# Hybrid decoder layer: eleven weight subtractions moved to GpSimd, a one-column product written as another instruction, a minimum folded into the reduction before it

## The chip, the core and the metric

The kernel runs on one core of one Trainium2 chip. The metric is the device time in microseconds (us) of one execution. The kernel before took a median of 1356.11 us in three runs (1355.26 to 1356.71); less is better. A core has five engines that work side by side and meet by semaphores: TensorE (PE in the profile; its weight loads have a row of their own, PEld), VectorE (DVE), ScalarE (ACT), GpSimd (POOL) and SyncE (SP, which only issues DMAs here). Each takes its instructions in a fixed order.

## The reference, cut to what matters

One decoder layer on 1024 tokens of width 1024, in float32. The part that the change touches:

```python
xn = rmsnorm(x, norm_mix_w[l])
proj = xn @ w_in[l]
da_q, da_k, da_v, sw_q, sw_k, sw_v, g_da, g_sw = split_cols(proj)
y_da = diff_attention(da_q, da_k, da_v, lam, lam_init, subln_w[l])
y_sw = sliding_window_attention(sw_q, sw_k, sw_v, sinks[l])
merged = sigmoid(g_da) * (y_da @ w_br_da[l]) + sigmoid(g_sw) * (y_sw @ w_br_sw[l])
x = x + merged @ w_mix_out[l]
...
# diff_attention, per head and block of 128 queries: two softmaxes, then
a = p[:, :, 0] - lam * p[:, :, 1]
# sliding_window_attention, per group of 4 heads: window of 128 keys plus a sink logit
p = softmax(concatenate([logits, sink], axis=-1), axis=-1)[..., :-1]
```

After it come a gated feed-forward part with a causal convolution and a last normalisation, which the change does not touch.

## The kernel before, in words

Every large matrix product is done in three passes on numbers split in two: a weight block `raw` of 128x1024 comes by DMA, ScalarE copies its high part `wh` (L129), VectorE subtracts to get the low part `wl` (L131), and TensorE then runs high x high, high x low and low x high (L150 to L152). `load_w` does the loading and splitting; `ahead` takes the next entry of a list of sources made in `plan` and calls it, so that a block is split one block ahead of its use. An entry may carry a third element, the engine of the subtraction; without one it is VectorE.

The input projection has 34 column blocks. Two gate blocks are done early and three in pairs; the last eleven gate blocks (23 to 33) are kept back and computed during attention: `back_half` runs one half (128x512) of one block, 24 matmuls, copies it to SBUF and stores it to DRAM (L494 to L498). Which halves follow which attention step is written out by hand in `HALVES`. They give TensorE something to do while the softmaxes run.

Attention has six units. Units 0 to 3 are the differential heads, each of eight steps (`da_step`): step i forms the scores of 128 queries against (i+1)x128 keys for two score maps (L568), adds the distance bias and takes the row minimum in one custom VectorE instruction (L572, followed by an instruction that reads out its accumulator), exponentiates on ScalarE (L573), forms the factor of the second map from a reciprocal and a one-column product (L576, L577), subtracts the maps on VectorE (L578), transposes the result on TensorE in groups of up to four blocks (L584) and splits it (ScalarE L586, VectorE L587). Every second step `da_av` multiplies with the values (L596 to L598). `da_norm` leaves the head's normalisation to the next unit's steps: L616 to L620 and the transposes of L173. Score tiles, transpose tiles and gate tiles have two buffers each in PSUM, so L568 can write a score tile only when the L572 two tiles before has read it, and L584 a transpose tile only when L587 (or ScalarE's copy) has read the one two before.

Units 4 and 5 are the sliding window in groups of four heads (`sw_step`, 8 steps each): scores (L656), bias and row minimum for each of the heads (L659), the minimum with the negated sinks (L661), the sink's distance from it (L662), exponentials (L663, L665), sum and reciprocal (L666, L667), normalising (L670: three heads on VectorE, the fourth on GpSimd), transposes (L677), splitting (L680, L681), product with the values (L687), and L689 to L694 to gather the result. GpSimd otherwise clears score tiles (L551), takes the -1/2 power (L167) and does L620 in this stretch; before it and after it, it does large products and sums (L385, L725).

The order in which one engine gets its instructions is not that of the source: the framework's scheduler orders them when the program is built, from dependencies, buffers, priorities and its own cost estimates; so single gate matmuls stand among those of the attention. After that the order is fixed. SP's queue issues the loads, among them the next `raw` (L119), which waits until one of three buffers has been read.

Of the kernel before, what the change touches and what calls it, by code (L numbers as in the profile page):

```python
# [13 lines left out]
ALU = mybir.AluOpType  # L14
# [6 lines left out]
KC = D // P  # L21
# [21 lines left out]
class Trunk:  # L43
# [173 lines left out]
    def plan(self):  # L217

        self.kind = {m: "q" if m < 4 or 12 <= m < 16 else "k" if m < 8 or m == 16 else "v" if m < 18 else "g" for m in range(34)}


        self.plain = [0, 4, 8, 18, 20]
        self.pairs = [(1, 5), (9, 2), (6, 10), (3, 7), (11, 12), (13, 16), (17, 14), (15, 19), (21, 22)]
        gates = list(range(23, 34))
        self.back = []
        todo = [(m, hf) for m in gates for hf in range(2)]
        for steps in HALVES:
            self.back.append([[todo.pop(0) for _ in range(n)] for n in steps])
        assert not todo
        src = [(self.w_in[m], KC) for m in self.plain]  # L230
        src += [((self.w_in[a], self.w_in[b]), "pair") for a, b in self.pairs]
        src += [(self.w_in[m], KC) for m in gates]
        src += [(self.w_br[m], KC) for m in range(KC)]
        self.mix_order = [m for k in range(4) for m in (k, k + 4)]
        src += [(self.w_mix[m], KC) for m in self.mix_order]
        src += [((self.w_up[j], self.w_up[j + NF]), "pair") for j in range(NF)]


        n, n2 = N1 // 2, NF - N1 - 8
        self.pieces = [(m, c) for m0 in (4, 0) for c in range(2) for m in range(m0, m0 + 4)]  # L240
        src += [(self.w_dn[m:m + 2, :, n * c:n * c + n, :].rearrange("m p k c -> p m k c"), 2 * n) for m, c in self.pieces[::2]]
        pairs = [(self.w_dn[m, :, N1:N1 + 8, :], self.w_dn[m + 4, :, N1:N1 + 8, :]) for m in range(4)]
        src.insert(len(src) - 2, (pairs[0], "sums"))
        src += [(self.w_dn[m, :, N1:N1 + 8, :], 8) for m in range(4)]
        src += [(pairs[0], "rest")] + [(p, "pair", True, 1) for p in pairs[1:]]
        src += [(self.w_dn[m, :, N1 + 8:, :], n2) for _ in range(2) for m in range(KC)]
        self.wsrc, self.wq, self.deep = src, [], False
# [306 lines left out]
    def da_step(self, h, i, st, aT):  # L554
        nc, ap = self.nc, self.ap
        q, k = st
        slope = 4.0 ** -(h + 1)
        w = (i + 1) * P

        lo = P if w == 640 else 0  # L560
        cuts = ((0, 256),) if i == 0 else ((0, w),) if w <= H2 else ((0, H2 - lo), (H2 - lo, w))
        pr = []
        for c in range(2):
            sc = self.tl(self.psS, [P, T], "sc")
            qs = q[c][:, i * P:(i + 1) * P]
            for part in range(2):
                for n0, n1 in cuts:
                    nc.tensor.matmul(sc[:, lo + n0:lo + n1], qs, k[c][part][:, n0:n1], start=part == 0, stop=part == 1)  # L568
            L = self.tl(ap, [P, T], "L", bufs=4)
            s = self.tl(self.st, [P, 4], "sm", bufs=8)  # L570
            o = 896 - i * P
            nc.vector.tensor_tensor_reduce(L[:, :w], sc[:, lo:lo + w], self.bias[:, o:o + w], slope, 3e38, ALU.add, ALU.min, s[:, 0:1])  # L572
            nc.scalar.activation(L[:, :w], L[:, :w], AF.Exp, bias=s[:, 0:1], scale=-1.0, accum_out=s[:, 1:2] if c else self.s0[:, i:i + 1])  # L573
            pr.append(L)

        nc.vector.reciprocal(s[:, 2:3], s[:, 1:2])  # L576
        nc.vector.tensor_scalar(s[:, 3:4], self.s0[:, i:i + 1], s[:, 2:3], self.neglam, ALU.mult, ALU.mult)  # L577
        nc.vector.scalar_tensor_tensor(pr[0][:, :w], pr[1][:, :w], s[:, 3:4], pr[0][:, :w], ALU.mult, ALU.add)  # L578
        qo = (i % 2) * P
        for j0 in range(0, i + 1, 4):  # L580
            nj = min(4, i + 1 - j0)
            ps = self.tl(self.psT, [P, 4, P], "t")
            for j in range(nj):
                nc.tensor.transpose(ps[:, j, :], pr[0][:, (j0 + j) * P:(j0 + j + 1) * P], self.ident)  # L584
            hi, lo = aT[j0 // 4, 0], aT[j0 // 4, 1]
            nc.scalar.copy(hi[:, :nj, qo:qo + P], ps[:, :nj, :])  # L586
            nc.vector.tensor_tensor(lo[:, :nj, qo:qo + P], ps[:, :nj, :], hi[:, :nj, qo:qo + P].bitcast(F32), ALU.subtract)  # L587
# [57 lines left out]
    def sw_step(self, g, n, st):  # L645
        nc, ap = self.nc, self.ap
        q, k = st
        k0 = max(n - 1, 0) * P
        w = P if n == 0 else 256
        bo = T + (P if n == 0 else 0)  # L650
        sc = self.tl(self.psS, [P, 4, 256], "sc")
        s = self.tl(self.st, [P, 4, 4], "sw", bufs=4)
        L = self.tl(ap, [P, 4, 256], "L", bufs=4)
        for h in range(4):
            for part in range(2):
                nc.tensor.matmul(sc[:, h, :], q[h][:, n * P:(n + 1) * P], k[part][:, k0:k0 + 256], start=part == 0, stop=part == 1)  # L656
        for h in range(4):
            slope = 2.0 ** -(4 * g + h + 1)
            nc.vector.tensor_tensor_reduce(L[:, h, :w], sc[:, h, :w], self.bias[:, bo:bo + w], slope, 3e38, ALU.add, ALU.min, s[:, 0, h:h + 1])  # L659
        sink = self.vecs[:, C_SINK + 4 * g:C_SINK + 4 * g + 4]  # L660
        nc.vector.tensor_tensor(s[:, 0, :], s[:, 0, :], self.nsink[:, 4 * g:4 * g + 4], ALU.min)  # L661
        nc.vector.tensor_tensor(s[:, 1, :], s[:, 0, :], sink, ALU.add)  # L662
        nc.scalar.activation(s[:, 1, :], s[:, 1, :], AF.Exp)  # L663
        for h in range(4):
            nc.scalar.activation(L[:, h, :w], L[:, h, :w], AF.Exp, bias=s[:, 0, h:h + 1], scale=-1.0, accum_out=s[:, 2, h:h + 1])  # L665
        nc.vector.tensor_tensor(s[:, 2, :], s[:, 2, :], s[:, 1, :], ALU.add)  # L666
        self.last = nc.vector.reciprocal(s[:, 3, :], s[:, 2, :])  # L667
        for h in range(4):
            eng = nc.gpsimd if h in (3,) else nc.vector
            eng.tensor_scalar(L[:, h, :w], L[:, h, :w], s[:, 3, h:h + 1], None, ALU.mult)  # L670
        po = self.tl(self.psT, [P, H2], "t")
        nblk = w // P
        parts = []
        for b in range(nblk):
            ps = self.tl(self.psT, [P, 4, P], "t")
            for h in range(4):
                nc.tensor.transpose(ps[:, h, :], L[:, h, b * P:(b + 1) * P], self.ident)  # L677
            pt = self.tl(ap, [P, 2, 4, P], "aT", F32R, bufs=5)
            hi, lo = pt[:, 0], pt[:, 1]
            nc.scalar.copy(hi, ps)  # L680
            nc.vector.tensor_tensor(lo, ps, hi.bitcast(F32), ALU.subtract)  # L681
            parts.append((hi, lo))
        for b, (hi, lo) in enumerate(parts):
            kb = k0 // P + b
            va = self.vsw[kb // 4][:, kb % 4, g]
            for m, pt in enumerate((hi, lo)):
                nc.tensor.matmul(po, va, pt, start=b == 0 and m == 0, stop=b == nblk - 1 and m == 1)  # L687
        t = self.tl(self.gpool, [P, 4, P], "g", bufs=2)[0:64]
        nc.scalar.copy(t, po[64:128].rearrange("p (h q) -> p h q", h=4))  # L689
        pv = po[0:64].rearrange("p (c e q) -> p c e q", c=2, e=2)  # L690
        tv = t.rearrange("p (c e) q -> p c e q", e=2)
        y = self.tl(ap, [P, 2, P], "ys", bufs=3)
        for e in range(2):
            nc.vector.tensor_tensor(y[64 * e:64 * e + 64], pv[:, :, e], tv[:, :, e], ALU.add)  # L694
        self.store(self.yd[4 + 2 * g:6 + 2 * g, :, n * P:(n + 1) * P].rearrange("c p q -> p c q"), y)
# [515 lines left out]
```

## Time and profile before

| | |
|---|---|
| median of three runs | 1356.11 us (1355.26 to 1356.71) |
| the profiled execution | 1356.2 us, of which 1354.3 us are the span of its instructions |
| granted TensorE clock | 0.996 of full speed |
| busy over the span | PE 1335.0 us (99%), DVE 1009.8 us (75%), ACT 603.9 us (45%), POOL 483.1 us (36%) |

Times in the profile are counted from the span's first instruction. In a timeline row stand the start, the busy time, the engine, the source line, the operation with the tile it writes and those it reads, their shapes and how many instructions are merged into the row; in brackets the idle time of the engine before it and what ended that. In a table of stretches stand first and last time, length, and then for each engine its busy time with the number of instructions. In a row of a group stand the form, the count, the busy time of all and the mean in ns of one. A TensorE instruction's end is modelled, and one overlaps the next, so its starts say more than its busy time.

### The profile page before, as it was taken

Reading aid. Unit: us, or ns where it says so; the run is one execution under the profiler, and the core shown is the slowest. Engines: PE = TensorE matmul, PEld = TensorE weight load, DVE = VectorE, ACT = ScalarE, POOL = GpSimd, SP = SyncE. Lnnn points to the kernel's source line nnn. Section 1 sums busy time; section 2 is a strip of 40 time slices with the busy share of each in tenths; the row PEclk is TensorE's granted clock in tenths of the full one; section 3 lists DMA queues with packets and bytes.
Section 4 is the critical chain, followed back from the end, with each engine's and each line's share of the span. In section 5 each row is a group of like instructions: output and inputs, shape, how many; then the busy total and the mean of one; then the engine's idle time right before and its main releaser. Section 6 shows DMA issues by size and latency. Waiting matters only on the chain.

```text
span 1354.3 us, 17160 instructions
## 1 busy us (share of the span) xinstructions
PE 1335.0 (99%) x6304; PEld 1103.6 (81%) x6304; DVE 1009.8 (75%) x1454; ACT 603.9 (45%) x942; POOL 483.1 (36%) x350
## 2 busy tenths in 40 slices
PE   7999999999999999999999999999999999999997
PEld 6888888888887777878888888888888888888886
DVE  8846775388898875355689888888888898986454
ACT  8422232376667664334444334433443345433343
POOL 0436651010102125741455565555555611231011
PEclk9999999999999999999999999999999999999999
DMA  6334443966554235334422222122212248651342
GB/s 255 140 113 164 143 156 114 272 174 175 156 133 144 77 116 219 117 119 136 166 82 88 71 91 94 62 79 93 93 63 83 92 141 311 215 177 64 94 134 85
DMA packets 62470, 179.50 MB, mean 133 GB/s; under 512 B 6833, under 2 KB 15153, under 8 KB 62385
## 3 DMA queue, kind: packets, MB, share of 16 engines
q1 hardware_dynamic: 50928, 160.98, 36.7%
q10 hardware_dynamic: 11456, 17.41, 3.5%
q8 instruction: 50, 0.82, 0.2%
q14 instruction: 36, 0.29, 0.1%
HBM read 129.61 MB, written 48.76 MB: 132 GB/s over the span
## 4 chain that ended last, share of the span: by engine, by line
PE 62%; DVE 17%; POOL 7%; issue 7%; DMA 4%; ACT 3%; POOLq 0%; DVEq 0%; SPq 0%; ACTq 0%
PE t L836 7%; PE t L837 7%; PE t L835 7%; POOL us L965 3%; PE y L996 3%; PE d L996 3%; PE sc L568 3%; PE g L150 2%; PE g L151 2%; DVE c L958 2%; PE g L152 2%; DVE wl L112 2%; DMA gr<-gd 2%; PE sc L151 2%; PE sc L152 2%
## 5 line engine op out<-in xcount | busy, mean ns | idle before, releaser
L970 ACT ACTIVATE c<-us,vecs 128x1024 f32<-128x1024 f32 x44 | 54.8, 1248 | 163.2 <-POOL us L965 160.0
L965 POOL TENSOR_TENSOR us<-us,rstd 128x1024 f32<-128x1024 f32 x42 | 100.7, 2414 | 52.8 <-DVE wl L131 34.3
L110 ACT CAST sh<-sf 128x1024 fp32r<-128x1024 f32 x62 | 64.9, 1051 | 106.2 <-POOL sf L97 61.8
L129 ACT CAST wh<-raw 128x1024 fp32r<-128x1024 f32 (+2 forms) x60 | 60.7, 1012 | 104.8 <-PE sc L151 33.1
L971 DVE SCALAR_TENSOR_TENSOR c<-us,vecs,c 128x1024 f32<-128x1024 f32 x44 | 67.1, 1527 | 51.9 <-ACT c L970 51.9
L131 DVE TENSOR_TENSOR wl<-raw,wh 128x1024 fp32r<-128x1024 f32 (+2 forms) x60 | 75.3, 1256 | 39.1 <-ACT wh L129 29.3
L96 POOL TENSOR_TENSOR sf<-rv 128x512 f32<-128x512 f32 x30 | 42.5, 1417 | 166.7 <-DMA rv<-in_w_up 73.2
L112 DVE TENSOR_TENSOR sl<-sf,sh 128x1024 fp32r<-128x1024 f32 x62 | 88.3, 1426 | 8.2 <-ACT sh L110 8.2
L167 POOL TENSOR_TENSOR rs<-ms,mhalf 128x8 f32<-128x8 f32 (+2 forms) x9 | 14.5, 1614 | 159.1 <-DVE ms L165 148.5
L150 PE MATMUL g<-xh,wh 128*128 128x512 f32 x176 | 70.7, 402 | 0.1
L152 PE MATMUL g<-xh,wl 128*128 128x512 f32 x176 | 70.4, 400 | 0.0
L151 PE MATMUL g<-xl,wh 128*128 128x512 f32 x176 | 70.4, 400 | 0.0
L98 POOL TENSOR_TENSOR sf<-raw,rv 128x512 f32<-128x512 f32 x30 | 41.6, 1386 | 59.9 <-DVE sl L112 59.9
L572 DVE CUSTOM_DVE_ANT_0 L<-sc,bias 128x128 f32<-128x128 f32 (+7 forms) x64 | 47.7, 752 | 17.4 <-PE sc L568 14.1
L551 POOL MEMSET aT<- 128x128 f32 x32 | 6.1, 204 | 152.0 <-PE t L597 101.6
L573 ACT ACTIVATE L<-L,sm 128x128 f32<-128x128 f32 (+7 forms) x64 | 49.6, 778 | 20.7 <-DVE sm L572 18.2
L97 POOL TENSOR_TENSOR sf<-sf,raw 128x512 f32<-128x512 f32 x31 | 58.0, 1870 | 1.6
L972 DVE SCALAR_TENSOR_TENSOR c<-us,vecs,c 128x1024 f32<-128x1024 f32 x44 | 56.2, 1279 | 0.6
L725 POOL TENSOR_TENSOR gr<-gr,rstd 128x1024 f32<-128x1024 f32 x16 | 39.4, 2467 | 41.4 <-DMA gr<-gd 41.2
L112 DVE TENSOR_TENSOR wl<-raw,wh 128x1024 fp32r<-128x1024 f32 (+1 forms) x35 | 52.8, 1508 | 0.1
L151 PE MATMUL sc<-ml,wh 128*128 128x512 f32 x128 | 50.1, 391 | 0.6 <-DVE ml L746 0.6
L568 PE MATMUL sc<-u,u 128*128 128x512 f32 (+2 forms) x192 | 49.8, 359 | 0.1
(444 smaller groups left out, 4351.4 us busy)
## 6 DMA issues: line engine op xcount, KB each, us to landing
u<-qd SPq DMA_DIRECT2D x72, 256.0 KB, 6.1
raw<-in_w_down SPq DMA_DIRECT2D x27, 512.0 KB, 3.7
raw<-in_w_in SPq DMA_DIRECT2D x25, 512.0 KB, 4.4
hr<-hd SPq DMA_DIRECT2D x50, 256.0 KB, 5.3
raw<-in_w_up SPq DMA_DIRECT2D x23, 512.0 KB, 3.6
hd<-c SPq DMA_DIRECT2D x22, 512.0 KB, 2.8
rv<-in_w_up SPq DMA_DIRECT2D x21, 512.0 KB, 3.5
gr<-gd SPq DMA_DIRECT2D x16, 512.0 KB, 3.6
```

What stands on the lines that cost most here:

```text
L112: nc.vector.tensor_tensor(lo, src, hi.bitcast(F32), ALU.subtract)
L131: self.lo = (eng or nc.vector).tensor_tensor(wl, raw, wh.bitcast(F32), ALU.subtract)
L150: nc.tensor.matmul(ps, wh[:, kc + o, :], ah, start=first and n == 0, stop=False)
L151: nc.tensor.matmul(ps, wh[:, kc + o, :], al, start=False, stop=False)
L152: nc.tensor.matmul(ps, wl[:, kc + o, :], ah, start=False, stop=last and n == len(kcs) - 1)
L568: nc.tensor.matmul(sc[:, lo + n0:lo + n1], qs, k[c][part][:, n0:n1], start=part == 0, stop=part == 1)
L835: nc.tensor.matmul(ps, ah[:, k, :], bh, start=first and n == 0, stop=False, skip_group_check=skip)
L836: nc.tensor.matmul(ps, ah[:, k, :], bl, start=False, stop=False, skip_group_check=skip)
L837: nc.tensor.matmul(ps, al[:, k, :], bh, start=False, stop=last and n == len(ks) - 1, skip_group_check=skip)
L965: i = (nc.vector if m % NF == 0 else nc.gpsimd).tensor_tensor(us[:, 2:], us[:, 2:], self.rstd, ALU.mult)
L971: nc.vector.scalar_tensor_tensor(c, us[:, 1:T + 1], cw[1], c, ALU.mult, ALU.add)
L996: nc.tensor.matmul(ps, v[:, n, :], x, start=n == i == 0, stop=n == len(js) - 1 and i == 2)
```

## The change

Three edits. The list entries of the eleven gate blocks name GpSimd as the engine of the subtraction at L131. The one-column product at L577, until now a `tensor_scalar` of one column with two per-partition scalars, becomes a `scalar_tensor_tensor` of two columns with one such scalar. And the reduction at L659 gets the column of the negated sink as the value its minimum begins with, in place of the constant 3e38, and the separate minimum at L661 goes.

```diff
-        src += [(self.w_in[m], KC) for m in gates]
+        src += [(self.w_in[m], KC, self.nc.gpsimd) for m in gates]
...
-        nc.vector.tensor_scalar(s[:, 3:4], self.s0[:, i:i + 1], s[:, 2:3], self.neglam, ALU.mult, ALU.mult)
+        nc.vector.scalar_tensor_tensor(s[:, 3:4], self.s0[:, i:i + 1], self.neglam, s[:, 2:3], ALU.mult, ALU.mult)
...
-            nc.vector.tensor_tensor_reduce(L[:, h, :w], sc[:, h, :w], self.bias[:, bo:bo + w], slope, 3e38, ALU.add, ALU.min, s[:, 0, h:h + 1])
+            nc.vector.tensor_tensor_reduce(L[:, h, :w], sc[:, h, :w], self.bias[:, bo:bo + w], slope, self.nsink[:, 4 * g + h:4 * g + h + 1], ALU.add, ALU.min, s[:, 0, h:h + 1])
         sink = self.vecs[:, C_SINK + 4 * g:C_SINK + 4 * g + 4]
-        nc.vector.tensor_tensor(s[:, 0, :], s[:, 0, :], self.nsink[:, 4 * g:4 * g + 4], ALU.min)
```

## The prediction

> **What bounds the kernel now.** I read the page first, then the table of stretches over attention, then the moved line in the same stretches, then the timelines at the places that it leads to.
>
> ```profile
> span 1354.3 us, 17160 instructions
> PE 1335.0 (99%) x6304; PEld 1103.6 (81%) x6304; DVE 1009.8 (75%) x1454; ACT 603.9 (45%) x942; POOL 483.1 (36%) x350
> ...
> 223.00:266.00 43.00, 42.91 (x196) 35.38 (x195) 12.53 (x22) 8.04 (x13) 0.85 (x5) 1.00 0.79 234
> 266.00:397.00 131.00, 130.93 (x832) 114.66 (x831) 114.92 (x298) 90.43 (x211) 10.81 (x33) 1.00 0.60 160
> 397.00:497.00 100.00, 98.17 (x552) 79.17 (x551) 85.95 (x315) 70.25 (x207) 17.53 (x18) 1.00 0.35 106
> ```
>
> The columns after the length are PE, PEld, DVE, ACT and POOL, then the granted clock and the DMAs. PE sets the time. In the four differential heads (266 to 397) it is idle 0.07 us, in the sliding window (397 to 497) 1.83 us. VectorE is second, busy 88% and 86% there, GpSimd idle almost throughout. So relief for VectorE pays only where PE stands waiting for it, and a delay of VectorE costs as soon as it exceeds its lead over PE.
>
> The same stretches for L131 alone (the last one ends before the first block of w_br, which stays on VectorE):
>
> ```profile
> 223.00:266.00 43.00, 4.90 (x4) 1.00 0.79 234
> 266.00:397.00 131.00, 4.88 (x4) 1.00 0.60 160
> 397.00:493.00 96.00, 3.62 (x3) 1.00 0.34 105
> ```
>
> These are the eleven: 1.22 us each, four in a stretch where VectorE is busy 12.53 of 43 us, four among the heads, three in the window.
>
> **Part one, the subtraction on GpSimd.** What does a 128x1024 operation with two inputs in SBUF cost there, and what does it do to VectorE?
>
> ```profile
> 198.36 2.41 POOL L385 TENSOR_TENSOR us<-us,rstd 128x1024 f32<-128x1024 f32 x1 [0.52 <-DVE us L401]
> 198.45 3.40 DVE L112 TENSOR_TENSOR sl<-sf,sh 128x1024 fp32r<-128x1024 f32 x1 [0.17 <-ACT sh L110]
> ```
>
> GpSimd takes 2.41 us. The VectorE subtraction that starts 0.09 us after it has the form of L131, 1.22 us, but takes 3.40: it ends at 201.85, which is GpSimd's end (200.77) plus 1.08. So a VectorE operation that reads two SBUF tensors does not run beside such a GpSimd operation; it waits for its end and then runs whole. The other way round too:
>
> ```profile
> 476.83 1.20 DVE L131 TENSOR_TENSOR wl<-raw,wh 128x1024 fp32r<-128x1024 f32 x1
> 477.11 1.71 POOL L670 TENSOR_SCALAR L<-L,sw 128x256 f32<-128x256 f32 x1 [9.19 <-DVE sw L667]
> 479.70 0.99 POOL L670 TENSOR_SCALAR L<-L,sw 128x256 f32<-128x256 f32 x1 [0.88 <-PE t L677]
> ```
>
> GpSimd's L670 takes 1.71 us behind L131 and 0.99 without. So a moved subtraction takes 1.22 us off VectorE and can hold it for up to 2.41 if one of its two-input operations comes up meanwhile (L578, L617, L662, L666): from 1.22 us early to 1.19 late for each.
>
> The first four cost nothing: VectorE is idle 71% of that stretch, which is the cover; without it each would fall under the bounds just given. For the heads I place the hold in the trace. GpSimd can start when ScalarE's copy of `wh` ends. Second of the four:
>
> ```profile
> 321.82 1.07 ACT L129 CAST wh<-raw 128x1024 fp32r<-128x1024 f32 x1
> 322.53 1.15 DVE L578 SCALAR_TENSOR_TENSOR L<-L,sm,L 128x896 f32<-128x896 f32 x1
> 323.60 0.16 DVE L617 TENSOR_TENSOR r<-r 128x8 f32<-128x8 f32 x1
> 323.67 1.22 DVE L131 TENSOR_TENSOR wl<-raw,wh 128x1024 fp32r<-128x1024 f32 x1
> 324.88 0.27 DVE L572 CUSTOM_DVE_ANT_0 L<-sc,bias 128x128 f32<-128x128 f32 x1
> 325.49 0.40 PE L568 MATMUL sc<-u,u 128*128 128x256 f32 x2
> ```
>
> The copy ends at 322.89, in the middle of L578; GpSimd gets in when that ends, about 323.6, and holds until 326.0. Next on VectorE is L617, eight columns wide, but with two SBUF inputs: it waits. It ends at about 326.1 where L131 ended at 324.89, and L572 follows 1.2 late, reading its score tile until 326.4. L568 at 325.49 writes the tile that this L572 frees: PE stands about 1.0 us, and behind it in PE's order stand gate matmuls that were ready. The third:
>
> ```profile
> 358.54 1.07 ACT L129 CAST wh<-raw 128x1024 fp32r<-128x1024 f32 x1
> 359.19 1.28 DVE L578 SCALAR_TENSOR_TENSOR L<-L,sm,L 128x1024 f32<-128x1024 f32 x1
> 360.39 0.16 DVE L617 TENSOR_TENSOR r<-r 128x8 f32<-128x8 f32 x1
> 360.47 1.22 DVE L131 TENSOR_TENSOR wl<-raw,wh 128x1024 fp32r<-128x1024 f32 x1
> 361.60 1.15 DVE L587 TENSOR_TENSOR aT<-t,aT 128x512 fp32r<-128x512 f32 x2
> 362.66 0.60 PE L584 MATMUL t<-ident,L 128*128 128x128 f32 x4
> ```
>
> The same pattern: hold from 360.4 to 362.8, L617 behind it, L587 from 361.60 to about 362.9, and the transposes at 362.66, which need the tile that the first L587 frees (361.60 plus half of 1.15), 1.2 late. The fourth:
>
> ```profile
> 392.18 1.15 DVE L578 SCALAR_TENSOR_TENSOR L<-L,sm,L 128x896 f32<-128x896 f32 x1
> 393.62 0.15 DVE L617 TENSOR_TENSOR r<-r 128x8 f32<-128x8 f32 x1
> 396.41 1.28 DVE L578 SCALAR_TENSOR_TENSOR L<-L,sm,L 128x1024 f32<-128x1024 f32 x1
> 397.87 1.04 PE L584 MATMUL t<-ident,L 128*128 128x128 f32 x8
> ```
>
> Hold from 393.3 to 395.7, L617 ends 2.1 late of which the missing L131 returns 1.2: L578 ends 0.9 late, at 398.6 instead of 397.69, and the transposes at 397.87 wait 0.7. The first of the four I take as even: a hold that begins anywhere takes half of 2.41 on average, and 1.22 is saved. Heads together: 0 + 1.0 + 1.2 + 0.7 = +2.9 us; bounds -0.1 (PE's idle time there, all of it) and 4 x 1.19 = +4.8.
>
> In the window:
>
> ```profile
> 434.16 0.35 DVE L670 TENSOR_SCALAR L<-L,sw 128x256 f32<-128x256 f32 x1
> 434.83 1.29 DVE L670 TENSOR_SCALAR L<-L,sw 128x256 f32<-128x256 f32 x3
> 434.99 0.99 POOL L670 TENSOR_SCALAR L<-L,sw 128x256 f32<-128x256 f32 x1 [1.69 <-PE t L677]
> 436.05 1.21 DVE L131 TENSOR_TENSOR wl<-raw,wh 128x1024 fp32r<-128x1024 f32 x1
> 437.18 1.28 DVE L681 TENSOR_TENSOR aT<-t,aT 128x512 fp32r<-128x512 f32 x2
> 492.42 1.28 PE L677 MATMUL t<-ident,L 128*128 128x128 f32 x4 [0.27 <-DVE L L670]
> ```
>
> Here GpSimd's L670 is done at 435.98, the subtraction follows until 438.4, and VectorE's next work is L681, whose one input is in PSUM: no hold, 1.2 us gained. PE's waits for VectorE are at places like the last row: four transposes in 1.28 us where four take 0.60 above, and 0.27 idle before. GpSimd's own L670 may queue up to 2.41 behind a subtraction, with the transposes L677 waiting for it; GpSimd is busy 17.53 of 100 us, so for three blocks I take 0.
>
> A rule against even that, row first: three L670 beside GpSimd's L670 took 1.29 us, 0.43 each against 0.35 alone; none waited for GpSimd's end at 435.98, or the last would end at 436.7 instead of 436.12. The Trainium skill (SBUF — State Buffer, "Who interferes with whom") counts VectorE's `tensor_scalar` in its two-port fast mode among what a GpSimd instruction blocks for its whole length; by it the sum would be 3.6 higher (below). The row decides against it for a one-input GpSimd instruction; no row shows a two-input one.
>
> **Part two, L577.** In the heads:
>
> ```profile
> L577 DVE TENSOR_SCALAR sm<-s,sm,neglam 128x1 f32<-128x1 f32 x32 | 8.7, 271 | 0.3
> L587 DVE TENSOR_TENSOR aT<-t,aT 128x512 fp32r<-128x512 f32 x22 | 14.9, 687 | 2.2 <-ACT aT L586 2.1
> L578 DVE SCALAR_TENSOR_TENSOR L<-L,sm,L 128x512 f32<-128x512 f32 x4 | 3.0, 746 | 0.0
> ```
>
> L578 has one per-partition scalar more than L587 and takes 59 ns more at equal size: I price such a scalar at 59. The new L577 has two columns and one scalar: the four-column two-input L661 below (158) plus 59 is 217, so 54 less, 32 times: 1.7 us off VectorE (bounds 0 and 32 x (271 - 158) = 3.6). It lies on the chain to L578, but PE idles 0.07 us: I take -0.1. The new form has two SBUF inputs, so it too can be held.
>
> **Part three, the minimum.** In the window:
>
> ```profile
> L659 DVE CUSTOM_DVE_ANT_0 L<-sc,bias 128x256 f32<-128x256 f32 x56 | 21.7, 418 | 1.6 <-PE sc L656 1.6
> L661 DVE TENSOR_TENSOR sw<-sw,nsink 128x4 f32<-128x4 f32 x16 | 2.5, 158 | 0.1
> ```
>
> 16 x 158 = 2.5 us go; 64 reductions (56 and 8 narrower) gain a scalar, 64 x 59 = 3.8 (bounds 0 and twice that, 7.6). VectorE pays 1.3. What is gained is a wait: a head's exponential need no longer wait for all four heads and L661, only for its own reduction.
>
> Window together: VectorE loses 3.6 and gets 1.3 back, and the chain is shorter; of PE's idle 1.83 I take it all, and nothing of what overlapping matmuls hide: -1.8, with bounds -4.5 (as much again, and the 0.95 of the last row) and +3.6 (three holds of 1.2). No queue is passed by a DMA; SP's `raw` load waits for the subtraction's end, which moves by at most 1.2 late and often early, with blocks split over 10 us ahead.
>
> **Sum:** +2.9 - 0.1 - 1.8 = +1.0 on the profiled execution's own 1356.2 (1354.3 of span, 1.9 around it), which is 0.1 above the median of the runs: 1357.1 us.
>
> **The rivals.**
> - Faster: the scheduler's new order puts the holds beside one-input operations (in the heads L572 and L587 are most of VectorE's time). For it: the window's rows; against it: L578 and L617 follow each other at every place that I looked at. Then 0 - 0.1 - 3.6 (twice the idle) = -3.7: 1352.5.
> - Slower: one mechanism, the hold, at all seven dense blocks, each at its full 1.19, with VectorE's lead gone so that PE pays all: 8.3 - 0.1 = +8.2, 1364.4. It decides once more than about four of the seven meet a two-input operation early. For it: each step has several (L578, L617, the new L577; L662, L666); against: the window's rows at 436.
> - The page's rule as a mechanism: a GpSimd subtraction stops the fast L670 too, in all three window blocks: 1357.1 + 3 x 1.2 = 1360.7.
> - Nothing on PE's path changes: holds and gains vanish in PE's order, 1356.2.
>
> **How the numbers follow.** A measurement of this kernel tells 0.2%, 2.7 us, from no change. Forecast 0.42 (own range 1354.5 to 1360: 0.02 faster, 0.32 same, 0.08 slower); faster 0.22 (0.18 faster, 0.04 same); slower 0.20; the page's rule 0.08 (0.02 same, 0.06 slower); nothing 0.08 (same). Together faster 0.20, same 0.46, slower 0.34. The range leaves out half of the slower rival and the far end of the faster: 1352 to 1362.5.
>
> **What would show it.** L131 on GpSimd at 2.4 us each; in the heads L617, L578 or L577 lengthened to up to 2.4 us behind it, and PE's busy time in the heads below all but 0.1; L577 near 217 ns; L659 near 477; PE's idle time in the window smaller. It is wrong if no VectorE row is lengthened beside the new subtractions, if L659 keeps 418, or if PE's order changes so much that waits of other kinds appear.

## The result, and the profile after

The changed kernel takes a median of 1362.51 us in six runs (1360.42 to 1365.5), the kernel before 1356.41 us in six runs on the same chip (1355.26 to 1357.39): ratio 1.0047, 95% interval [1.0034, 1.006], so 6.1 us slower. The profiled execution took 1363.76 us with a span of 1361.9. Of its source, the lines behind L661 have a number one smaller than before (L669 is before's L670, L686 its L687).

The head of the page of the changed kernel, and two stretches of attention with the columns explained above:

```profile
span 1361.9 us, 17127 instructions
...
PE 1335.7 (98%) x6304; PEld 1102.0 (81%) x6304; DVE 1011.0 (74%) x1427; ACT 604.0 (44%) x942; POOL 511.2 (38%) x361
```

```profile
266.00:397.00 131.00, 128.26 (x798) 109.81 (x797) 113.16 (x290) 87.63 (x207) 19.43 (x36) 1.00 0.58 156
397.00:505.00 108.00, 104.75 (x600) 85.51 (x599) 90.28 (x302) 74.46 (x213) 26.25 (x23) 1.00 0.36 107
```

TensorE does the same 6304 instructions in about the same busy time (1335.7 against 1335.0 us). What has grown is its idle time: 2.74 us among the heads where it was 0.07, and 3.25 us in the window where it was 1.83. VectorE has the 27 instructions less that the diff takes away (x1427 against x1454) but a busy time 1.2 us larger, so something on it runs longer. What TensorE waited for from 223 to 505 us (us in total, number of waits, longest), first in the changed kernel, then in the kernel before:

```profile
PE sc L568 <- DVE sm L572: 2.4, 2, 1.5
PE sc L568 <- DMA u<-qd: 1.5, 1, 1.5
PE t L686 <- DVE aT L680: 1.4, 1, 1.4
PE t L686 <- DVE v L643: 1.1, 1, 1.1
PE g L150 <- ACT g L497: 0.6, 1, 0.6
```

```profile
PE t L687 <- DVE aT L681: 0.4, 2, 0.2
PE t L677 <- DVE L L670: 0.4, 2, 0.3
PE t L677 <- POOL L L670: 0.2, 1, 0.2
```

Waits of 1.0 us in all have become 7.0, five of those in the three lines where VectorE is late. All in all TensorE is idle 7.5 us from 223 to 505 us where it was idle 2.0; that is 5.5 of the 7.6 us between the two profiled spans. The single prices are as predicted. All instructions of a line in the changed kernel, with minimum, median and maximum in ns:

```profile
L577 DVE SCALAR_TENSOR_TENSOR sm<-s,neglam,sm x32: 208/216/2373, 270.3 to 396.9; 128x1 f32<-128x1 f32 x32
L659 DVE CUSTOM_DVE_ANT_0 L<-sc,bias,nsink x64: 324/475/485, 400.2 to 496.8; 128x256 f32<-128x256 f32 x56, 128x128 f32<-128x128 f32 x8
L131 POOL TENSOR_TENSOR wl<-raw,wh x11: 2370/2389/2557, 226.9 to 478.8; 128x1024 fp32r<-128x1024 f32 x11
```

The maximum of L577 stands out, eleven times its median. The timeline of the changed kernel at four of the eleven subtractions says why:

```profile
291.21 2.56 POOL L131 TENSOR_TENSOR wl<-raw,wh 128x1024 fp32r<-128x1024 f32 x1 [0.39 <-ACT wh L129]
291.45 2.34 DVE L617 TENSOR_TENSOR r<-r 128x8 f32<-128x8 f32 x1
294.05 0.51 PE L568 MATMUL sc<-u,u 128*128 128x256 f32 x2 [0.92 <-DVE sm L572]
331.95 2.38 POOL L131 TENSOR_TENSOR wl<-raw,wh 128x1024 fp32r<-128x1024 f32 x1 [4.41 <-ACT wh L129]
331.97 2.37 DVE L577 SCALAR_TENSOR_TENSOR sm<-s,neglam,sm 128x1 f32<-128x1 f32 x1
408.72 2.37 POOL L131 TENSOR_TENSOR wl<-raw,wh 128x1024 fp32r<-128x1024 f32 x1 [3.94 <-ACT wh L129]
409.10 2.03 DVE L165 TENSOR_SCALAR ms<-r 128x8 f32<-128x8 f32 x1
436.42 2.37 POOL L131 TENSOR_TENSOR wl<-raw,wh 128x1024 fp32r<-128x1024 f32 x1
436.94 2.00 DVE L669 TENSOR_SCALAR L<-L,sw 128x256 f32<-128x256 f32 x1
```

Each of these VectorE instructions begins while GpSimd subtracts and ends when GpSimd ends: 291.45 + 2.34 is 293.79, GpSimd's end 293.77. Alone, L617 takes 0.16 us and L670 0.35. The two waits for L572 and those for L643 and L680 in the list above follow just behind these four places (TensorE's next instruction starts at 294.05, 335.1, 411.9 and 439.6). A fifth, an L577 at 369.24, is held for 1.26 us. The two last of those shown are not of the kind that the prediction counted as held: L165 and L669 are `tensor_scalar`, with one input in SBUF.

But the hold was not the whole difference. Set side by side, some 575 of TensorE's 6304 matmuls stand in another place of its order than before, all of them between 269 and 519 us, in attention and just behind it, although no edit touches TensorE. So there were three theories: the **order** (the scheduler, given other costs and another engine for eleven instructions, made another order for all engines), the **hold** (GpSimd's subtractions stop VectorE), and SyncE's **late load** (the `raw` load waits for the longer subtraction, and the loads queued behind it, among them that of `u`, come late: the 1.5 us of L568 above).

### The profile page after: what moved, and what is told of

Read it like the earlier page. It is cut to its first block, busy times and chain, and to the rows that moved or that the text cites. A ratio compares the mean times of both kernels' runs of the same rounds, so it can differ in the third digit from the quotient of the medians.

```text
span 1361.9 us, 17127 instructions
## 1 busy us (share of the span) xinstructions
PE 1335.7 (98%) x6304; PEld 1102.0 (81%) x6304; DVE 1011.0 (74%) x1427; ACT 604.0 (44%) x942; POOL 511.2 (38%) x361
## 4 chain that ended last, share of the span: by engine, by line
PE 66%; DVE 18%; issue 6%; POOL 4%; DMA 3%; ACT 2%; POOLq 0%; SPq 0%; DVEq 0%; ACTq 0%
PE t L836 6%; PE t L835 6%; PE t L834 6%; POOL us L964 4%; PE y L995 3%; PE d L995 3%; PE g L151 3%; PE g L152 3%; PE g L150 3%; PE sc L152 3%; PE sc L150 3%; PE sc L151 3%; DVE wl L112 3%; DVE c L957 2%; PE sc L568 2%
## 5 line engine op out<-in xcount | busy, mean ns | idle before, releaser
L131 DVE TENSOR_TENSOR wl<-raw,wh 128x1024 fp32r<-128x1024 f32 (+2 forms) x49 | 64.1, 1309 | 23.8 <-ACT wh L129 23.5
L150 PE MATMUL g<-xh,wh 128*128 128x512 f32 x176 | 70.4, 400 | 0.6 <-ACT g L497 0.6
L151 PE MATMUL g<-xl,wh 128*128 128x512 f32 x176 | 70.7, 402 | 0.0
L152 PE MATMUL g<-xh,wl 128*128 128x512 f32 x176 | 70.3, 399 | 0.0
L572 DVE CUSTOM_DVE_ANT_0 L<-sc,bias 128x128 f32<-128x128 f32 (+7 forms) x64 | 47.7, 753 | 21.0 <-PE sc L568 18.1
L724 POOL TENSOR_TENSOR gr<-gr,rstd 128x1024 f32<-128x1024 f32 x16 | 42.3, 2647 | 38.0 <-DMA gr<-gd 37.5
L568 PE MATMUL sc<-u,u 128*128 128x512 f32 (+2 forms) x192 | 49.6, 359 | 3.9 <-DVE sm L572 2.4
L150 PE MATMUL sc<-mh,wh 128*128 128x512 f32 x128 | 49.8, 389 | 0.0
L151 PE MATMUL sc<-ml,wh 128*128 128x512 f32 x128 | 49.8, 389 | 0.0
```

The source lines that it names most:

```text
L150: nc.tensor.matmul(ps, wh[:, kc + o, :], ah, start=first and n == 0, stop=False)
L151: nc.tensor.matmul(ps, wh[:, kc + o, :], al, start=False, stop=False)
L152: nc.tensor.matmul(ps, wl[:, kc + o, :], ah, start=False, stop=last and n == len(kcs) - 1)
```

## The experiments

In all of them the ratio is to the kernel before on the same chip, whose median was 1354.2 to 1354.9 us there; a difference in us is one of medians, and the ratio isn't that of the medians (for e1 it is 1.0067, the medians give 1.0060).

### The three edits alone

Each kernel has a part of the diff shown above: the list entries (e1), the line L577 (e2), the lines L659 and L661 (e3), and both of the last (e4).

e1_gates:

> Only the eleven subtractions on GpSimd, L577 and L661 as before. If GpSimd's hold on two-input VectorE work and SyncE's wait for the longer subtraction are the cause: most of the loss, ratio 1.0035 to 1.005 (+4.5 to +7 us), and in the trace L617 or L578 (no longer L577, which has one tensor input again) lengthened to 2.2 to 2.5 us behind a POOL L131 in the heads. If the order that the scheduler makes, or the other two edits, are the cause: within 0.15% of before.

e2_product:

> Only the one-column product as scalar-tensor-tensor. If its price alone counts: L577 at 0.21 to 0.22 us in place of 0.271, PE hardly waits for it, so within 0.15% of before. If the new order of the heads costs (some 390 of 6247 TensorE rows stand elsewhere): slower by 0.15% or more without any GpSimd subtraction.

e3_minimum:

> Only the minimum that begins with the sink's column. By a per-partition scalar's price of 59 ns: L659 at 0.477, VectorE 1.3 us busier in the window, the time within 0.15% of before or slightly below. If the scalar costs nothing: L659 at 0.418 and up to 2 us faster.

e4_product_and_minimum:

> Both small edits without the subtractions. If the three edits add: the sum of the two single ones, and the changed kernel minus this one equals the subtractions alone (+4.5 to +7 us). If the subtractions only hurt together with the new L577, this and the kernel with the subtractions alone are both near before.

| kernel | median, us | ratio and interval |
|---|---|---|
| e1, subtractions on GpSimd | 1362.37 | 1.0067 [1.0055, 1.0079] |
| e2, the product | 1360.83 | 1.0047 [1.0035, 1.0059] |
| e3, the minimum | 1356.68 | 1.002 [1.0011, 1.0028] |
| e4, product and minimum | 1358.65 | 1.003 [1.0019, 1.0041] |

Every edit alone makes the kernel slower, and they don't add: 8.2 + 6.6 + 2.5 us would be 17, and the three together cost 6.1; product and minimum together cost less than the product alone. Of what was expected, e1 is on the side of the hold but above its range (in its trace an L578 of 1.28 us takes 3.17 behind a subtraction), e2 is on the side of the order, e3 is slower than either of its cases, and e4 fits neither of its two: the changed kernel is only 1.6 us slower than it. The product is the strange one. Its instruction became 55 ns cheaper, moved nowhere, and cost 6.6 us. The part of it that can do this is the order: some 380 of TensorE's matmuls stand elsewhere in e2.

### Order and instruction taken apart

The order can be held by hand. A kernel builds the program of the one whose order is wanted, notes the place of every instruction, then builds the program whose instructions are wanted and ties each pair of neighbours on an engine in the noted order. The tie is one of issue only, nothing waits for it on the chip. An instruction that changes its engine isn't tied and takes a place of its own. In the traces TensorE's matmuls and ScalarE's instructions start in exactly the order of before in e5 and e7 to e10, of e2 in e6, of e1 in e11, and of the changed kernel in e12 to e14.

```diff
+        traced = [x for x in nc.cur_bb.bb.instructions if x.name not in skip and "Boundary" not in type(x).__name__]
+        if order is not None:
+            for e in ENGINES:
+                mine = sorted((place[k][1], k) for k, x in enumerate(traced) if place[k][0] == e and x.engine == e and place[k][1] is not None)
+                for (_, a), (_, b) in zip(mine, mine[1:]):
+                    tc.add_manual_dep(traced[b], traced[a].name, mybir.DependencyInfo(mybir.DependencyClass.NoSync, mybir.DependencyReason.DATA), reason="order")
...
+    order, place, _, _ = _build(ins, *(False, False, False))
+    _, _, nc, out = _build(ins, *(False, True, False), order, place)
```

(The last two lines are those of e5: order of before, instructions with the product's edit.)

> The scalar-tensor-tensor form of L577 alone, with every engine held to the order in which before issues its instructions (the order is computed from before's own program and every pair of neighbours on an engine is tied). Nothing but the 32 instructions of L577 differs from before. If the new order of the instructions caused the 6.6 us of the product alone (theory: order): ratio 0.998 to 1.0015. If the instruction itself costs them, by its price or by being held behind GpSimd (rival: instruction): 1.0035 to 1.006 again.

> The counterpart: before's tensor-scalar at L577, with every engine held to the order that the product's edit produced. No instruction differs from before, only the order. Order: 1.0035 to 1.006, as with the product alone. Instruction: 0.9985 to 1.0015.

e5 measured 0.9998 [0.9989, 1.0007], 1354.53 us; e6 1.0048 [1.0036, 1.0061], 1361.57 us. The new instruction in the old order costs nothing, the old instruction in the new order costs all: the price of the edit is the order alone.

How can an order cost so much? One place of several is near the end of the window. TensorE's timeline in e6 and, at the same work, in e5:

```profile
493.03 1.23 PE L687 MATMUL t<-aT,v 128*128 128x512 f32 x3
494.48 0.51 PE L687 MATMUL t<-aT,v 128*128 128x512 f32 x1 [0.23 <-DVE aT L681]
495.64 1.28 PE L677 MATMUL t<-ident,L 128*128 128x128 f32 x4 [0.65 <-DVE L L670]
496.90 0.80 PE L150 MATMUL g<-xh,wh 128*128 128x512 f32 x1
497.49 0.63 PE L151 MATMUL g<-xl,wh 128*128 128x512 f32 x1
```

```profile
489.57 0.48 PE L150 MATMUL g<-xh,wh 128*128 128x512 f32 x1
489.89 0.67 PE L687 MATMUL t<-aT,v 128*128 128x512 f32 x2
490.39 0.39 PE L151 MATMUL g<-xl,wh 128*128 128x512 f32 x1
490.62 0.39 PE L152 MATMUL g<-xh,wl 128*128 128x512 f32 x1
490.85 0.99 PE L687 MATMUL t<-aT,v 128*128 128x512 f32 x2
492.10 1.28 PE L677 MATMUL t<-ident,L 128*128 128x128 f32 x4 [0.26 <-DVE L L670]
```

In e5 three gate matmuls (L150 to L152) stand between the L687 and cover VectorE's work on L681 and L670. In e6 they stand a few places earlier, ahead of the L677 before, and TensorE waits bare: L677 starts 1.16 us after the L687 before it, of which 0.65 is idle by the record. Both kernels do the same matmuls in the whole; only their places differ. After this wait the granted clock falls for 3.4 us (see the end), which makes the L151 last 0.63 us where it lasts 0.39 in e5.

This is not one rule for the whole order. Counted at equal places among the heads, e6 has issued up to 10 gate matmuls fewer than before, e11 (below) up to 16 and the changed kernel up to 20; in the window it is at times more and at times fewer. At 519 us of e5, where the orders agree again, e6 is 6.5 us behind. The place shown, the clock behind it and the held instruction told under e11, which e6 has too, make up more than half of that; the rest is spread over attention and wasn't traced to single waits.

### Part one in before's order

> The 11 subtractions of the gates on GpSimd, every other instruction of every engine in before's order; the 11 take places of their own in GpSimd's stream. Order: the gates alone cost 8.2 us with a new order, so most of it goes: 0.999 to 1.002, within about 3 us of before. Rival (the hold of GpSimd and VectorE and SyncE's longer wait for the raw buffer): these stay whatever the order is, some 1.5 us for a held instruction, twice, and 1.4 us for the late load: 1.003 to 1.0065.

> All three edits, the instructions that before also has in before's order (the 11 subtractions take their own places on GpSimd, the dropped minimum is left out). This is the changed kernel's arithmetic without its new order. Order: 0.998 to 1.001. Hold and SyncE's wait: 1.003 to 1.006, no better than the changed kernel as it stands (1.0047).

e7 measured 1.0029 [1.0018, 1.0041], 1358.35 us; e8 1.0035 [1.0023, 1.0047], 1359.8 us. With the order held, half of part one's 8.2 us stays, 4.0 us, between the two ranges. All three edits together still cost 5.4: e8 lies in the range of the hold, and for the changed kernel before's order repairs nothing that could be measured. e7 is the case that the prediction had worked out, the subtractions moved and everything else in its place. Its timeline at the second of the four among the heads and at the second in the window, and the group of L670:

```profile
322.70 2.96 POOL L131 TENSOR_TENSOR wl<-raw,wh 128x1024 fp32r<-128x1024 f32 x1 [0.30 <-ACT wh L129]
323.32 2.35 DVE L617 TENSOR_TENSOR r<-r 128x8 f32<-128x8 f32 x1
451.95 2.35 POOL L131 TENSOR_TENSOR wl<-raw,wh 128x1024 fp32r<-128x1024 f32 x1
451.62 2.77 DVE L670 TENSOR_SCALAR L<-L,sw 128x128 f32<-128x128 f32 x3
454.44 0.44 PE L677 MATMUL t<-ident,L 128*128 128x128 f32 x2 [1.57 <-DVE L L670]
```

```profile
L670 DVE TENSOR_SCALAR L<-L,sw x48: 274/372/2375, 403.9 to 494.9; 128x256 f32<-128x256 f32 x42, 128x128 f32<-128x128 f32 x6
```

The L617 is held as forecast, to 325.67. The other is the last of three L670, which end at 454.39 (451.62 + 2.77) where GpSimd's subtraction ends at 454.30; it is the maximum of its group, 2.375 us, and the transposes that read its output stand until GpSimd is done. In the kernel before the same group had a maximum of 578 ns, beside GpSimd's own L670.

I compared the starts of TensorE's instructions after equal amounts of work in e7 and before. e7 falls back by 0.9 us at 326, 0.8 at 364, 0.35 at 399 and 1.8 at 454, each time at a held VectorE instruction, and gains 1.0 us elsewhere in the window. That is 2.9 us in all; the profiled execution was 1.0 us faster than e7's median, so it fits, but the rest of the 4.0 us has no place. So four of the eleven subtractions should carry the loss. Two kernels with before's order split them:

```diff
-        src += [(self.w_in[m], KC) for m in gates]
+        src += [(self.w_in[m], KC, self.nc.gpsimd) if n in GATES else (self.w_in[m], KC) for n, m in enumerate(gates)]
...
+    _, _, nc, out = _build(ins, *({0, 1, 2, 3, 4, 8, 10}, False, False), order, place)
```

> As e7_gates_old_order (before's order held on every engine), but the four subtractions beside which TensorE lost time there (those of 322.7, 360.3, 393.9 and 452.0 us, the sixth, seventh, eighth and tenth) stay on VectorE; seven are on GpSimd. Hold: the four carried the loss, +0.9, +0.8, +0.35 and +1.8 us in the progress of TensorE, so 0.998 to 1.001. Rival (moving work to GpSimd costs whatever it meets, by the 1.2 us that each weight comes later): seven elevenths of e7's 4.0 us, 1.0015 to 1.0025.

> The counterpart: only those four subtractions on GpSimd, before's order held. Hold: the whole of e7's loss or a little more, 1.002 to 1.004. Rival: four elevenths of it, 1.0005 to 1.0015.

e9 measured 1.0004 [0.9995, 1.0013], 1354.61 us; e9b 1.0036 [1.0023, 1.0048], 1359.77 us. The four carry all of it, the seven nothing that could be measured, although one of the seven holds an L578 for 0.6 us; the rival, a cost for each moved subtraction, falls. (That e9b costs 5.2 us and e7 4.0 is within the noise; e9b's trace also has a spell of half clock there, see the end.) The window's row in e5 (before's order, none moved), e7 (all), and e9 (the seven):

```profile
397.00:505.00 108.00, 106.20 (x588) 85.85 (x587) 89.09 (x318) 75.34 (x214) 22.21 (x20) 1.00 0.37 117
```

```profile
397.00:505.00 108.00, 104.85 (x585) 85.14 (x584) 88.35 (x318) 72.53 (x212) 26.77 (x25) 1.00 0.39 119
```

```profile
397.00:505.00 108.00, 106.58 (x593) 86.86 (x592) 88.82 (x317) 76.05 (x215) 26.29 (x22) 1.00 0.37 117
```

TensorE's idle time in the window is 1.80 us with no subtraction moved, 3.15 with all, 1.42 with the seven. So these single executions show a gain from taking work off VectorE, about 0.4 us of idle time, but it is too small to be measured in the whole.

### Part three in before's order

> Part three alone (the minimum begins with the sink's column, L661 dropped), every instruction that before also has in before's order. With a new order it cost 2.5 us (1.002). Order: 0.9985 to 1.0007. Instruction (64 times 59 ns more at L659 against 16 times 158 ns less at L661, on VectorE where a product waits for it): 1.001 to 1.003.

e10 measured 1.0012 [1.0003, 1.002], 1356.19 us: 1.7 us slower. The median lies in the range of "instruction", but the interval reaches down into that of "order". The instruction seems to cost a little, and the 2.5 us of e3 are not shown to hold an order's share. Where the 1.7 us are lost isn't shown either: in e10's trace TensorE is 0.9 us behind e5 at 500 us and level with it at 525.

### The changed kernel's own order

> The changed kernel with its own order on every engine, but the 11 subtractions back on VectorE, where they take places of their own. What it loses against before is the order (with parts two and three), what it gains against the changed kernel's 1.0047 is GpSimd's share (hold and SyncE's longer wait). Hold and SyncE's wait carry the changed kernel's loss, 1.6 us at 291, 1.6 at 333, 1.4 at 409 and 1.4 at 259: 0.9995 to 1.0015. Order carries it: 1.003 to 1.006.

> The changed kernel itself, on the chip of the next three, so that they can be set against it: 1.0035 to 1.006, as in the first comparison (1.0047).

> The changed kernel in its own order, with the first two subtractions of the gates back on VectorE, so that SyncE's load of the raw buffer (at 242.9 us) isn't behind GpSimd's second one. SyncE's late load costs what TensorE's wait for u at 257.0 shows: that wait of 1.7 us goes, and the ratio falls by 0.001 against the changed kernel's. Rival (the load is hidden, the wait has another cause): the wait stays and so does the ratio.

> The changed kernel in its own order, with the five subtractions beside which a VectorE instruction was held (291.2, 331.9, 368.1, 408.7 and 436.4 us) back on VectorE; six stay on GpSimd. Hold: the steps of 1.05, 1.1, 0.7 and 0.85 us in TensorE's progress go, 3.7 us, ratio 1.0015 to 1.003. Rival (the order costs the same whoever subtracts): 1.0035 to 1.0055.

| kernel, all in the changed kernel's order | median, us | ratio and interval |
|---|---|---|
| a1, the changed kernel, eleven on GpSimd | 1360.11 | 1.0044 [1.0031, 1.0056] |
| e13, the first two on VectorE | 1360.12 | 1.0039 [1.0025, 1.0053] |
| e14, the five held ones on VectorE, six on GpSimd | 1357.84 | 1.0022 [1.0013, 1.0031] |
| e12, all on VectorE | 1359.17 | 1.0036 [1.0024, 1.0049] |

e12 ran on another chip than the other three; each ratio is to before on its own chip. e12 came out in the range of the order, e14 in that of the hold. Without the five held subtractions half of the ratio's excess goes, 2.3 us (the two intervals just touch), and in e14's trace no VectorE instruction is lengthened beside a subtraction any more. With all subtractions on VectorE the order, with parts two and three, still costs 4.6 us. So by the medians the changed kernel's loss is 4.6 for the order and the other two parts, 1.7 given back by the six harmless subtractions (e14's 2.9), and 2.3 taken by the five held ones (a1's 5.2). Each of these three is uncertain by some 1.5 us, so the 1.7 given back is not shown, and in before's order the seven gave back nothing (e9); that e12 and e14 are both slower than before is not in doubt. Set against e8 this is the odd result of the whole: the moved work in the old order costs 5.4 us, the new order without the moved work 4.6, and both together, the changed kernel, 5.2.

e13's ratio is not to be told from a1's, and a1 shows why. TensorE's waits in a1 from 223 to 505 us, all of them:

```profile
PE sc L568 <- DVE sm L572: 2.4, 2, 1.5
PE t L686 <- DVE aT L680: 1.4, 1, 1.4
PE t L686 <- DVE v L643: 1.1, 1, 1.1
PE g L150 <- ACT g L497: 0.5, 1, 0.5
```

These are the changed kernel's own rows of above, to a tenth, but for the DMA: with the first two subtractions on GpSimd as there, the wait for `u` isn't there, though SyncE's load waits 5.1 us for the subtraction in both. Of the traces of all kernels that have these two on GpSimd, only that one shows the wait. So e13 had nothing to take away, and the late load falls as a cause of the lasting loss; the five held instructions are the same in both executions and in e13.

### Part one's order without its work

> Part one's order without its work: the 11 subtractions on VectorE, everything else in the order that part one alone produced; no instruction differs from before. Part one alone cost 8.2 us, and 4.0 in before's order. If order and hold add, the order costs 4.2 us: 1.002 to 1.0045. If all of the rest is GpSimd's too: 0.9985 to 1.0015.

e11 measured 1.0058 [1.0045, 1.007], 1362.34 us, against e1's 1.0067 with the same order. I had expected 1.002 to 1.0045 from adding; the order alone is worth 7.4 us of e1's 8.2. Hold and order do not add. A likely reason, which no run isolates, is that both eat the same lead of VectorE over TensorE: a hold where TensorE waits anyway costs little. Two of e11's rows of waits, from 223 to 535 us:

```profile
PE t L677 <- DVE L L670: 2.7, 3, 1.2
PE g L151 <- DVE yl L756: 2.3, 3, 1.7
```

The three of the first row lie in the second half of the window, at 447.9, 483.3 and 497.7 us, the last where e6 has its own. The longest of the second, 1.7 us just behind it, is something else. GpSimd's, VectorE's and TensorE's rows there, and then the same two instructions of GpSimd and VectorE in e2:

```profile
522.41 5.80 POOL L725 TENSOR_TENSOR gr<-gr,rstd 128x1024 f32<-128x1024 f32 x2 [12.50 <-DMA gr<-gd]
522.54 3.41 DVE L756 TENSOR_TENSOR yl<-yr,yh 128x1024 fp32r<-128x1024 f32 x1
526.00 0.50 PE L151 MATMUL g<-yl,wh 128*128 128x512 f32 x1 [1.66 <-DVE yl L756]
```

```profile
521.04 1.22 DVE L756 TENSOR_TENSOR yl<-yr,yh 128x1024 fp32r<-128x1024 f32 x1
521.27 5.64 POOL L725 TENSOR_TENSOR gr<-gr,rstd 128x1024 f32<-128x1024 f32 x2 [12.43 <-DMA gr<-gd]
```

It is a hold again, by a GpSimd product that no edit touches: the L756 (a subtraction of two tensors in SBUF, which makes a low part for the next stage) begins 0.13 us after the L725 and takes 3.41 us, 2.2 more than in e2, where it begins 0.23 us before the L725. e1 and e6 have the same held L756 and the same wait of 1.7 us; e2, with e6's order, hasn't. In e3 two earlier L756 are held behind the two earlier L725 of this stretch, from 502.6 us on, and TensorE waits 2.3 us. So part of what is called the order here is a hold that a shift of some tenths of a microsecond brings on or takes away.

No version beat both kernels. e5 (0.9998) and e9 (1.0004) are level with the kernel before.

## Why the prediction was wrong, point by point

- **What bounds the kernel** was right: TensorE's busy time is the same (1335.7 against 1335.0 us), and most of the loss is idle time of TensorE in attention, 5.5 of 7.6 us of span, of which 1.5 is the wait for `u` of that one execution.
- **The prices** were right: 2.39 us for GpSimd's subtraction (2.41 taken), 216 ns for L577 (217), 475 to 477 for L659 (477). That the new L577 could be held was said and came true twice in the changed kernel (2.37 and 1.26 us).
- **The hold among the heads**, "0 + 1.0 + 1.2 + 0.7 = +2.9 us", was right in its mechanism and places and some 0.9 us too large: in before's order (e7) it measured 0, 0.9, 0.8 and 0.35, 2.05 in all.
- **The window**, "-1.8", is the step that failed, and it failed in before's own order, in which the prediction had read its places. With the gains and losses of e7 the window's share of part one is +0.8 us. The sentence on L670 said that the row decides against a hold "for a one-input GpSimd instruction; no row shows a two-input one", and the sum has nothing for it. e7 shows the two-input one: L670 held for 2.375 us, 1.8 us lost by TensorE. That is the mechanism of the third rival, at one block of three. The Trainium skill (SBUF — State Buffer, "Who interferes with whom") says that whichever of the two begins first has the shared ports for its whole length; by it the L670 that begins 0.06 us into the subtraction can't end before it, and the trace agrees (454.39 against 454.30). And the 1.83 us of idle time that were to vanish did not: with the seven harmless subtractions moved, the idle time fell by 0.4 (e9).
- **Part two**, "-0.1", was right for the instruction (e5: 0.9998).
- **Part three**, the other half of the window's term, was priced right, but the gain in the wait that was to outweigh it didn't come: +1.7 us in before's order (e10).
- **SyncE's load**, counted as nothing, is not shown to cost anything that lasts (a1).
- **The sum** gave +1.0. In before's order its parts measured +4.0 for part one (e7), nothing for part two (e5) and +1.7 for part three (e10), and together +5.4 (e8). So nearly the whole error is there before any new order. By e7's trace and e10's median the window's terms are about 4.3 us too low (+0.8 and +1.7 for -1.8), the heads 0.9 too high, and about 1 us has no place.
- **The new order** is a term of its own that the sum lacks. The prediction priced it only as a gain, in the faster rival ("the scheduler's new order puts the holds beside one-input operations"), and named it as a loss without a price ("if PE's order changes so much that waits of other kinds appear"). It measured 7.2 us for part two (e6), 7.4 for part one (e11) and, with parts two and three, 4.6 in the changed kernel (e12). Since the old order (e8) and the new order without the moved work (e12) each give nearly the whole loss, the changed kernel's loss can't be divided between the two by adding.
- **The result**, 1362.51 us, lies just above the range's end of 1362.5 and near the slower rival's 1364.4, but that rival is not borne out: five of eleven subtractions held VectorE, not seven at full price, and by the medians they carry 2.3 of 5.2 us (a1, e14). The nearness is luck.

What stays open: why the scheduler, for a product that is 55 ns cheaper, puts the gate matmuls elsewhere, since its reasons are in no trace; where the rest of e6's loss in attention arises; and how much of the 1.7 us of part three is price.

## What to carry to other kernels

Where a scheduler makes the order, an edit is worth its own price plus that of the new order, and the second can be by far the larger: before an instruction is judged, tie the old order and run it, and do the reverse, the old instructions in the new order. Before work is moved to GpSimd, look at what comes up on VectorE while it runs, `tensor_scalar` as well as two-input operations in SBUF, and whether TensorE waits for that: in before's order seven of eleven such subtractions were free, and four cost 4 to 5 us. And read the places of covering work (here the gate matmuls) in the order itself, since an order that moves it by a few places looks as busy in the averages; tying it to the steps that it covers is the remedy to try, which no run here did alone.

## What the runs showed of the hardware

A one-input `tensor_scalar` on VectorE, even of eight columns, stands behind a two-input GpSimd operation until that ends (L165 2.03 us, L670 2.375 us), while beside GpSimd's one-input L670 the same instruction takes at most 578 ns: lengthened, but the one that begins 0.1 us into GpSimd's 0.99 us ends 0.3 us before GpSimd does. Of a two-input operation on each engine the one that begins first runs through, be it by 0.13 or 0.23 us (L725 and L756 in e11 and e2). And TensorE's granted clock has spells of one half that last 3.4 us. In e6, after the bare wait of above, it reads 0.50 from 496.8 to 500.2 us, and the mean over nine microseconds 0.81:

```profile
492.00:501.00 9.00, 7.64 (x26) 4.91 (x26) 5.83 (x12) 5.28 (x13) 0.98 (x1) 0.81 0.35 105
```

e2, which has the same order, has the spell at the same place. Most other executions, the kernel before's and e5's among them, have one such spell near 700 us, or none there; e6 has both. e9b has one at 455.6 us, just after the held L670, and e7, with the same hold at the same place, has none. I estimate that a spell costs half its length, 1.7 us, since the matmuls in it follow each other 0.43 us apart where it is 0.23 in e5. In e6 that is part of what the new order of part two costs; e2 has its spell in place of the one near 700 us. That a wait brings it on is only a guess.
